# Another token order in the second half of an output projection, late mixed factors, and factor stores issued by SyncE

## The chip, the cores and the metric

The kernel runs on one core of one Trainium2 chip. Its engines are TensorE (PE, matmuls; PEld loads the stationary operand), VectorE (DVE), ScalarE (ACT), GpSimd (POOL) and SyncE (SP, which only issues transfers). Each takes its own instructions strictly in order. The metric is the device time of one execution in microseconds (us), lower is better. Three executions of the kernel before took 1875.26, 1884.01 and 1888.64 us, median 1884.01 us.

## What is computed

One layer of a hybrid encoder on 1024 tokens of width 1024, all in float32. The change touches its last third only: the output projection, the norm after it and the SwiGLU network.

```python
def reference(x, c, ...):
    ...
        merged = (jax.nn.sigmoid(ga) * (y_a @ w_branch_a[l])
                  + jax.nn.sigmoid(gb) * (y_b @ w_branch_b[l]))
        x = x + g1 * (merged @ w_out[l])

        h = rmsnorm(x, ln2_g[l]) * (1.0 + sc2) + sh2
        f = (jax.nn.silu(h @ w_ffn_gate[l]) * (h @ w_ffn_up[l])) @ w_ffn_down[l]
        x = x + g2 * f
    return x
```

The hidden width of the SwiGLU network is 2816.

## The kernel before

**Precision.** Every float32 operand of a matmul is split into a high part (a copy rounded on ACT) and a low part (source minus high part, on DVE). A product is three matmuls: high by high, high by low, low by high. `split` does this for a 128x512 weight, `split_big` for an activation factor of 128x4x512. Wherever a factor is new, PE therefore waits first for an ACT copy, then for a DVE subtraction.

**Output projection (lines 1086 to 1158).** Two passes `ch` over 512 output columns each. A pass goes over 8 token tiles `i` of 128 tokens: 24 matmuls fill one PSUM bank `e`; DVE multiplies by the gate (`tm`, line 1131) and adds the residual (`x1`, line 1138). Tiles 0 to 3 are token half 0, tiles 4 to 7 token half 1. The inputs of the projection lie in four big buffers, `mh` and `mlo` for each half. In the second pass a row of `x1` is whole, so the norm follows: ACT squares with a sum (line 1142), POOL makes the inverse root (lines 115 and 116), ACT scales into `xn` (line 1146). Two tiles later PE transposes `xn` in 8 pieces (`tail_tr`, line 1020), and `tail_ev` evicts these with scale and shift into `h2b[e][n]`, in turn on ACT (line 1030) and DVE (line 1032). Here `e` is the feature half and `n` the token half.

**Entry of the SwiGLU network.** The gate and up products run as a Strassen scheme of the Winograd kind: 7 products instead of 8 for each of the 11 pairs `j` of 128-wide weight tiles. Its seven activation factors, each split into `rh[q]` and `rl[q]`, are made of the four blocks `h2b`. Factors 0 and 1 are the raw blocks of token half 0 (buffers `bh`, `bl`, which take over big buffers of `mh` and `mlo`); 2 is the raw block of feature half 1 and token half 1; 5, 4, 6 and 3 are sums and differences. `tail_f(i)` makes the mixed blocks in place, tile by tile: part 0 has three subtractions on DVE and one ACT copy, of 128x4x128 each, part 1 two more DVE subtractions. Part 1 overwrites the raw blocks of token half 0, so factors 0 and 1 have to be split before it.

**What sets the order.** A scheduler places the instructions of each engine from the order of the code and its own estimates of time. Between `i0` (line 1113, at the last tile) and `in_order(i0)` (line 1192) each engine keeps the order in which the code was written. Buffers come in rings: 3 for `raw` weight loads, 3 for `fs`, 8 PSUM banks.

**The loop over j (lines 1255 to 1287).** `strassen(j, 0, w_g)` makes the gate and `strassen(j, 1, w_u, hidden)` the up projection. When a quadrant of their product is ready, `hidden` makes seven factors of the hidden activation, and `put_f` splits each into an `fs` buffer (ACT, then DVE) and stores it to DRAM as `d_f[q, j]`, in the order q = 0, 3, 5, 4, 6, 1, 2. ACT issues these stores, and POOL issues those of the last j (j = 10). The weights `raw` are loaded by SP.

**The down projection (from line 1289).** It walks over seven products, q = 0 first. For each (q, j) SP loads `f` from `d_f[q, j]` (`get_f`, line 1301) and PE does 12 matmuls. SP also loads the weights `wd` (line 1310).

Of the kernel before, what the change touches and what calls it, by code (L numbers as in the profile page):

```python
# [8 lines left out]
F32 = mybir.dt.float32  # L9
F32R = mybir.dt.float32r  # L10
AF = mybir.ActivationFunctionType
# [5 lines left out]
P = 128  # L17
# [11 lines left out]
def block_kernel(tc, x, x_t, cols, ada_1, ada_2, ada_row, w_q, w_kv, w_v1, w_cg, w_a, w_b, w_o, w_g, w_u, w_d, out):  # L29
# [12 lines left out]
    def big():  # L42
        return bigp.tile([P, KT, 512], F32R, tag="big", bufs=4, name=nm("big"))
# [84 lines left out]
    def tt(eng, out, a, b, op):  # L128
        eng.tensor_tensor(out=out, in0=a, in1=b, op=op)  # L129
# [346 lines left out]
    pre = {}  # L476
# [520 lines left out]
    def split(src):  # L997

        hi = wp.tile([P, 512], F32R, tag="whi", bufs=8, name=nm("whi"))
        lo = wp.tile([P, 512], F32R, tag="wlo", bufs=8, name=nm("wlo"))  # L1000
        nc.scalar.activation(hi, src, AF.Copy)
        los.append(nc.vector.tensor_tensor(out=lo, in0=src, in1=hi.bitcast(F32), op=ALU.subtract))
        return hi, lo
# [4 lines left out]
    a2 = const.tile([P, 8], F32, name="a2")  # L1008
    nc.vector.scalar_tensor_tensor(out=a2, in0=mod[:, 3, :], scalar=1.0, in1=ln2, op0=ALU.add, op1=ALU.mult)

    def split_big(dh, dl, src):
        for k in range(0, src.shape[1], 2):
            nc.scalar.activation(dh[:, k:k + 2], src[:, k:k + 2], AF.Copy)
            tt(nc.vector, dl[:, k:k + 2], src[:, k:k + 2], dh[:, k:k + 2].bitcast(F32), ALU.subtract)

    def tail_tr(xn):
        trs = [bank() for g in range(2)]
        for g in range(2):
            for j in range(4):
                nc.tensor.transpose(trs[g][:, j * P:(j + 1) * P], xn[:, (4 * g + j) * P:(4 * g + j + 1) * P], ident)  # L1020
        return trs

    def tail_ev(i, trs, acts=(0, 2)):
        n, t0 = i // 4, (i % 4) * P
        for g in range(2):
            for j in range(4):
                k = 4 * g + j
                o, s = h2b[g][n][:, j, t0:t0 + P], trs[g][:, j * P:(j + 1) * P]
                if j in acts:
                    nc.scalar.activation(o, s, AF.Identity, scale=a2[:, k:k + 1], bias=mod[:, 2, k:k + 1])  # L1030
                else:
                    nc.vector.tensor_scalar(out=o, in0=s, scalar1=a2[:, k:k + 1], scalar2=mod[:, 2, k:k + 1],
                                            op0=ALU.mult, op1=ALU.add)

    def tail_f(i, qs=(0, 1)):

        t0 = (i % 4) * P
        b = lambda e, m: h2b[e][m][:, :, t0:t0 + P]
        if 0 in qs:
            h_, l_ = (r[:, :, t0:t0 + P] for r in (rh[2], rl[2]))  # L1040
            tt(nc.vector, b(0, 1), b(0, 1), b(0, 0), ALU.subtract)
            nc.scalar.activation(h_, b(1, 1), AF.Copy)
            tt(nc.vector, l_, b(1, 1), h_.bitcast(F32), ALU.subtract)
            tt(nc.vector, b(1, 1), b(1, 1), b(0, 1), ALU.subtract)
        if 1 in qs:
            tt(nc.vector, b(0, 0), b(1, 1), b(0, 0), ALU.subtract)
            tt(nc.vector, b(1, 0), b(1, 0), b(1, 1), ALU.subtract)

    def norm2_tail(i, xn):
        tail_ev(i, tail_tr(xn))  # L1050
        if i > 3:
            tail_f(i)

    NJ = NH // 2
    pq = {}
# [4 lines left out]
    def product(w, q):  # L1060
        ps = bank()
        prod(ps, w, q)
        return ps

    def two(sa, sb):
        return product(sa, 0), product(sb, 1)
# [20 lines left out]
    for ch in range(2):  # L1087
        w = [] if ch else list(w_pre)
        for j in range(len(w) // 2, 4):
            raw = load_raw(w_o[ch, j])  # L1090
            w += [split(raw[:, c * 512:(c + 1) * 512]) for c in range(len(w) % 2, 2)]
        if ch == 0:
            ws0, ws1 = [wt(q) for q in range(4)], [wsb(q) for q in range(3)]
            for src, ws in ((w_g, ws0), (w_u, ws1 + [None])):
                w_sums(load_raw(src[0]), load_raw(src[NJ]), *ws, nc.vector)
        if ch == 1:
            swx.close()
            rqs.close()
            sr2 = ExitStack()
            r2p = sr2.enter_context(tc.tile_pool(name="phr2", bufs=1, side="right", reuse_waits="tile"))  # L1100
            rh, rl = [None] * 7, [None] * 7
            rh[2], rl[2] = (r2p.tile([P, 4, 512], F32R, name=f"r{q}2") for q in "hl")
            s5 = ExitStack()
            hp = s5.enter_context(tc.tile_pool(name="phh", bufs=1, side="right", reuse_waits="tile"))

            h2t = {q: hp.tile([P, 4, 512], F32, name=f"h2b{q}") for q in ("01", "11", "00", "10")}
            h2b = [[h2t[f"{e}{n}"] for n in range(2)] for e in range(2)]
        cs = slice(ch * 512, ch * 512 + 512)
        for i in range(8):
            n, t0 = i // 4, (i % 4) * P  # L1110
            last = (ch, i) == (1, 7)
            if last:
                i0 = len(nc.cur_bb.bb.instructions)
                s00, s00b = halves(load_raw(w_g[0]))
            xi = dp.tile([P, 512], F32, tag="xr", bufs=2, name=nm("xr"))
            nc.scalar.dma_start(xi, x[i * P:(i + 1) * P, cs])
            ps = bank()
            for k in range(KT):
                if last and k == 4:
                    trs5 = tail_tr(tails.pop(0)[1])  # L1120
                nc.tensor.matmul(ps, mh[n][:, k, t0:t0 + P], w[k][0], start=(k == 0), stop=False)
                nc.tensor.matmul(ps, mh[n][:, k, t0:t0 + P], w[k][1], start=False, stop=False)
                nc.tensor.matmul(ps, mlo[n][:, k, t0:t0 + P], w[k][0], start=False, stop=(k == KT - 1))
            if last:
                tail_ev(5, trs5)
                tail_f(5)
                pq[1] = product(s00, 0)
                trs6 = tail_tr(tails.pop(0)[1])
                pq[2] = product(s00b, 1)
            tm = dp.tile([P, 512], F32, tag="tm", bufs=1, name=nm("tm"))  # L1130
            nc.vector.tensor_tensor(out=tm, in0=ps, in1=g1b[:, cs], op=ALU.mult)
            if ch == 0:
                nc.vector.tensor_tensor(out=tm, in0=tm, in1=xi, op=ALU.add)
                nc.scalar.dma_start(d_x1[i, :, cs], tm)
                continue
            x1 = dp.tile([P, D], F32, tag="x1", bufs=2, name=nm("x1"))
            nc.scalar.dma_start(x1[:, :512], d_x1[i, :, :512])
            nc.vector.tensor_tensor(out=x1[:, cs], in0=tm, in1=xi, op=ALU.add)
            nc.scalar.dma_start(d_x1[i, :, cs], x1[:, cs])
            ss = dp.tile([P, 1], F32, tag="ss", bufs=3, name=nm("ss"))  # L1140
            xn = dp.tile([P, D], F32, tag="xn", bufs=3, name=nm("xn"))
            nc.scalar.activation(xn, x1, AF.Square, accum_out=ss)  # L1142
            r = rstd_of(ss, 1.0 / D, dp, 1)
            if last:
                s01 = halves(load_raw(w_u[0]))
            nc.scalar.activation(xn, x1, AF.Copy, scale=r[:, 0:1])
            tails.append((i, xn))
            if last:
                tail_ev(6, trs6, (0,))
                tail_f(6)  # L1150
            elif len(tails) > 2:
                norm2_tail(*tails.pop(0))
            if i == 4:
                bh, bl = big(), big()
                rh[:2], rl[:2] = (bh[:, 0:4], bh[:, 4:8]), (bl[:, 0:4], bl[:, 4:8])
            if i == 5:
                for e in range(2):
                    split_big(bh[:, 4 * e:4 * e + 4], bl[:, 4 * e:4 * e + 4], h2b[e][0])


    pre = {}
    trs7 = tail_tr(tails.pop()[1])
    s6.close()

# [4 lines left out]
    for q in (6, 3):  # L1169
        rh[q] = ep.tile([P, 4, 512], F32R, name=f"rh{q}")  # L1170
        rl[q] = ep.tile([P, 4, 512], F32R, name=f"rl{q}")
    pre[0, 1] = two(*s01)
    sp2, sp1 = split(ws0[1]), split(ws0[0])
    x1p, x11 = wt(1), wt(0)
    nc.scalar.activation(x1p, pq[1], AF.Copy)
# [6 lines left out]
    pq[6] = product(sp2, 5)  # L1182
    split_big(rh[4], rl[4], h2b[0][1])
    pq[5] = product(sp1, 4)
    tail_f(7, (1,))
    pq[3] = product(split(ws0[3]), 2)
    sp3 = split(ws0[2])
    split_big(rh[6], rl[6], h2b[0][0])
    pq[7] = product(sp3, 6)
    sp4 = split(load_raw(w_g[NJ])[:, 512:])  # L1190
    split_big(rh[3], rl[3], h2b[1][0])
    in_order(i0)
    s5.close()
# [55 lines left out]
    def put_f(q, j, src):  # L1249
        fs = cp.tile([P, 2, 512], F32R, tag="fs", bufs=3, name=nm("fs"))  # L1250
        nc.scalar.activation(fs[:, 0], src, AF.Copy)
        tt(nc.vector, fs[:, 1], src, fs[:, 0].bitcast(F32), ALU.subtract)
        (nc.gpsimd if j == NJ - 1 else nc.scalar).dma_start(d_f[q, j], fs.rearrange("p a t -> p (a t)").bitcast(F32))

    for j in range(NJ):
        gate = strassen(j, 0, w_g)
# [242 lines left out]
```

## Time and profile before

| What | us |
|---|---|
| Median of three runs (lowest, highest) | 1884.01 (1875.26, 1888.64) |
| The profiled execution, whole | 1880.62 |
| Its span, first to last instruction | 1878.8 |
| PE busy in the span | 1817.9 (97%) |
| DVE, ACT, POOL busy | 1419.7, 867.3, 371.9 |
| Mean granted TensorE clock | 0.993 |
| Second pass of the output projection | about 1176 to 1224.6 |
| Entry of the SwiGLU network | about 1224.6 to 1274.3 |
| Loop over j | to 1663.9 |
| Down projection | 1664.7 to the end |

Times in the trace count from the start of the span. A row of the timeline has the start, the duration, the engine (with a q where its queue issues a transfer), the line, the operation, the names written and read, and in brackets how long the engine had been idle and what ended that. Matmuls overlap: at the full clock one that reads 128x512 starts 0.227 us after the one before, though each is shown as 0.39 us long.

### The profile page before, as it was taken

The numbers are of one execution on the slowest core, as the hardware profiler recorded it, in microseconds if no ns is written. First come the engines' busy times: TensorE is split into PE (matmuls) and PEld (weight loads), VectorE is DVE, ScalarE is ACT, GpSimd is POOL, SyncE is SP. The second block draws the span as 40 slices with busy tenths as digits, with TensorE's granted clock in tenths as the row PEclk, the third lists the DMA queues.
The fourth block names the chain that finished last, engine by engine and source line by source line (L and its number), as shares of the span: only waits on it lengthen the run. The fifth ranks groups of instructions, "written<-read, shape, count | busy, mean of one in ns | idle before, by whom it ended". The sixth has DMA issues, their size and how long they took to land.

```text
span 1878.8 us, 24981 instructions
## 1 busy us (share of the span) xinstructions
PE 1817.9 (97%) x8813; PEld 1507.3 (80%) x8813; DVE 1419.7 (76%) x2074; ACT 867.3 (46%) x1602; POOL 371.9 (20%) x280
## 2 busy tenths in 40 slices
PE   7899999999999999999998999989999999999999
PEld 5687778888878988887886787867888888888887
DVE  6774777779865999999999544489887778744776
ACT  4442553333344777777776321564444434422321
POOL 0043327423230000000000000004544344300000
PEclk9999999999999999999999999989999999999999
DMA  9689452227748665678563536314343334379766
GB/s 389 197 311 314 172 185 79 85 74 258 268 146 261 162 193 173 172 206 269 162 176 116 203 114 218 132 66 168 146 185 141 143 134 172 135 286 351 291 227 222
DMA packets 155196, 361.62 MB, mean 192 GB/s; under 512 B 15424, under 2 KB 52544, under 8 KB 152896
## 3 DMA queue, kind: packets, MB, share of 16 engines
q1 hardware_dynamic: 80224, 237.15, 38.1%
q10 hardware_dynamic: 73840, 119.22, 17.6%
q0 software_dynamic: 1008, 3.67, 0.5%
q8 instruction: 70, 1.15, 0.2%
q14 instruction: 54, 0.44, 0.1%
HBM read 245.15 MB, written 114.82 MB: 192 GB/s over the span
## 4 chain that ended last, share of the span: by engine, by line
PE 69%; DVE 16%; DMA 6%; ACT 4%; issue 3%; POOL 1%; ACTq 0%; SPq 0%; DVEq 0%; POOLq 0%
PE e L126 6%; PE e L125 6%; PE e L124 6%; PE pj L287 5%; PE pj L124 5%; PE pj L125 5%; PE pj L126 5%; PE e L1328 4%; PE e L1327 4%; PE e L1326 4%; DVE pt L744 3%; PE pj L819 3%; PE pj L821 3%; PE pj L820 3%; PE tr L760 2%
## 5 line engine op out<-in xcount | busy, mean ns | idle before, releaser
L744 DVE TENSOR_TENSOR_SCAN pt<-pt,dm 128x128 f32<-128x128 f32 (+7 forms) x128 | 171.5, 1344 | 7.9 <-ACT pt L739 7.6
L124 PE MATMUL e<-big,whi 128*128 128x512 f32 x352 | 138.9, 395 | 2.9 <-ACT c L1227 2.0
L125 PE MATMUL e<-big,whi 128*128 128x512 f32 x352 | 138.5, 393 | 0.8 <-DVE big L129 0.8
L126 PE MATMUL e<-big,wlo 128*128 128x512 f32 x352 | 138.5, 393 | 0.0
L129 DVE TENSOR_TENSOR c<-e,c 128x512 f32<-128x512 f32 x142 | 95.4, 687 | 53.4 <-PE e L126 50.9
L115 POOL TENSOR_SCALAR rs_m<-ss 128x1 f32<-128x1 f32 x8 | 2.4, 302 | 657.9 <-ACT xn L1142 657.9
L739 ACT ACTIVATE pt<-z,rq 128x512 f32<-128x512 f32 (+1 forms) x192 | 112.5, 586 | 42.3 <-PE z L738 17.9
L124 PE MATMUL pj<-big,whi 128*128 128x512 f32 x320 | 125.1, 391 | 0.4 <-DVE c L129 0.4
L125 PE MATMUL pj<-big,whi 128*128 128x512 f32 x320 | 124.7, 390 | 0.0
L126 PE MATMUL pj<-big,wlo 128*128 128x512 f32 x320 | 124.4, 390 | 0.0
L1326 PE MATMUL e<-whi,f 128*128 128x512 f32 (+1 forms) x319 | 121.8, 382 | 0.7 <-DMA f<-d_f 0.7
L1327 PE MATMUL e<-wlo,f 128*128 128x512 f32 (+1 forms) x319 | 121.8, 382 | 0.0
L1328 PE MATMUL e<-whi,f 128*128 128x512 f32 (+1 forms) x319 | 121.7, 382 | 0.0
L287 PE MATMUL pj<-whi,big 128*128 128x512 f32 x352 | 111.9, 405 | 5.3 <-DVE vs L402 2.9
L129 DVE TENSOR_TENSOR c<-pj,c 128x512 f32<-128x512 f32 x140 | 93.3, 683 | 29.0 <-PE pj L126 28.8
L129 DVE TENSOR_TENSOR wlo<-raw,whi 128x512 fp32r<-128x512 f32 x116 | 91.5, 792 | 30.5 <-ACT whi L460 30.5
L740 ACT ACTIVATE sg<-z,rq 128x512 f32<-128x512 f32 (+1 forms) x192 | 112.5, 587 | 1.1 <-PE tr L760 1.1
L460 ACT ACTIVATE whi<-raw 128x512 fp32r<-128x512 f32 x116 | 72.8, 633 | 86.9 <-PE pj L125 38.9
L129 POOL TENSOR_TENSOR ws<-raw,raw 128x512 f32<-128x512 f32 x40 | 56.2, 1405 | 277.3 <-DMA raw<-w_cg 165.1
L764 DVE TENSOR_TENSOR atl<-tr,ath 128x512 fp32r<-128x512 f32 (+1 forms) x192 | 100.5, 543 | 6.7 <-ACT ath L763 3.7
L125 PE MATMUL e<-rl,whi 128*128 128x512 f32 x264 | 103.6, 392 | 0.4 <-DVE rl L129 0.4
L126 PE MATMUL e<-rh,wlo 128*128 128x512 f32 x264 | 103.6, 392 | 0.0
(251 smaller groups left out, 5168.5 us busy)
## 6 DMA issues: line engine op xcount, KB each, us to landing
f<-d_f SPq DMA_DIRECT2D x77, 512.0 KB, 4.3
d_f<-fs ACTq DMA_DIRECT2D x70, 512.0 KB, 3.3
raw<-w_cg SPq DMA_DIRECT2D x40, 512.0 KB, 3.8
raw<-w_g SPq DMA_DIRECT2D x25, 512.0 KB, 3.4
raw<-w_u SPq DMA_DIRECT2D x25, 512.0 KB, 3.2
ad<-ada ACTq DMA_DIRECT2D x19, 512.0 KB, 4.4
ada<-ada SPq DMA_DIRECT2D x8, 1024.0 KB, 10.1
d_t<-ts SPq DMA_DIRECT2D x16, 512.0 KB, 4.3
```

What stands on the lines that cost most here:

```text
L124: nc.tensor.matmul(ps, wh[:, k, :], fh[:, k, :], start=(k == 0), stop=False)
L125: nc.tensor.matmul(ps, wh[:, k, :], fl[:, k, :], start=False, stop=False)
L126: nc.tensor.matmul(ps, wl[:, k, :], fh[:, k, :], start=False, stop=(k == 3))
L129: eng.tensor_tensor(out=out, in0=a, in1=b, op=op)
L287: nc.tensor.matmul(ps, a, b, start=(k == 0 and q == 0), stop=(k == KT - 1 and q == 2))
L739: nc.scalar.activation(pt[:, off + s0:off + s0 + m], z[:, :m], AF.Sigmoid, scale=rq[:, 1, i, h:h + 1])
L740: nc.scalar.activation(sg[:, s0:s0 + m], z[:, :m], AF.Sigmoid, scale=rq[:, 0, i, h:h + 1])
L744: nc.vector.tensor_tensor_scan(out=pt[:, rev], data0=pt[:, rev], data1=dm[:, rev], initial=0.0, op0=ALU.mult, op1=ALU.add)
L764: nc.vector.tensor_tensor(out=tl[:, :nb, c0:c0 + P], in0=src, in1=th[:, :nb, c0:c0 + P].bitcast(F32), op=ALU.subtract)
L1326: nc.tensor.matmul(o, sh, w[0][:, c], start=(j == 0), stop=False)
L1327: nc.tensor.matmul(o, sh, w[1][:, c], start=False, stop=False)
L1328: nc.tensor.matmul(o, sl, w[0][:, c], start=False, stop=(j == NJ - 1))
```

## The change

It has four parts. (1) The second pass takes the token tiles in the order 0, 4, 1, 5, 2, 3, 6, 7. The raw factors 0 and 1, which were split whole after tile 5, are split by token tile: tiles 0 and 1 after tile 3 of the new order, tile 2 after tile 6, tile 3 inside the last tile. (2) `tail_f` keeps only its part 0 at the tiles; the two subtractions of part 1, eight of 128x4x128, are two of 128x4x512 late in the entry, one ahead of each factor made of it. (3) The two products of the first up weight, `pre[0, 1]`, stand ahead of the transposes of the last tile instead of behind them, and one weight split stands earlier. (4) All 77 stores of the factors are issued by SP.

```diff
-    def split_big(dh, dl, src):
-        for k in range(0, src.shape[1], 2):
-            nc.scalar.activation(dh[:, k:k + 2], src[:, k:k + 2], AF.Copy)
-            tt(nc.vector, dl[:, k:k + 2], src[:, k:k + 2], dh[:, k:k + 2].bitcast(F32), ALU.subtract)
+    def split_big(dh, dl, src, t=None):
+
+        if t is None:
+            cuts = [(slice(k, k + 2), slice(0, 512)) for k in (0, 2)]
+        else:
+            cuts = [(slice(0, 4), slice(t * P, t * P + P))]
+        for c in cuts:
+            nc.scalar.activation(dh[:, *c], src[:, *c], AF.Copy)
+            tt(nc.vector, dl[:, *c], src[:, *c], dh[:, *c].bitcast(F32), ALU.subtract)
...
         if i > 3:
-            tail_f(i)
+            tail_f(i, (0,))
...
-        for i in range(8):
+        for i in (0, 4, 1, 5, 2, 3, 6, 7) if ch else range(8):
...
                 if last and k == 4:
-                    trs5 = tail_tr(tails.pop(0)[1])
+                    trs3 = tail_tr(tails.pop(0)[1])
...
             if last:
-                tail_ev(5, trs5)
-                tail_f(5)
+                tail_ev(3, trs3)
+                for e in range(2):
+                    split_big(bh[:, 4 * e:4 * e + 4], bl[:, 4 * e:4 * e + 4], h2b[e][0], 3)
                 pq[1] = product(s00, 0)
                 trs6 = tail_tr(tails.pop(0)[1])
                 pq[2] = product(s00b, 1)
...
             if last:
-                tail_ev(6, trs6, (0,))
-                tail_f(6)
+                tail_ev(6, trs6)
+                tail_f(6, (0,))
             elif len(tails) > 2:
                 norm2_tail(*tails.pop(0))
-            if i == 4:
-                bh, bl = big(), big()
-                rh[:2], rl[:2] = (bh[:, 0:4], bh[:, 4:8]), (bl[:, 0:4], bl[:, 4:8])
-            if i == 5:
+            if i in (3, 6):
+                if i == 3:
+                    bh, bl = big(), big()
+                    rh[:2], rl[:2] = (bh[:, 0:4], bh[:, 4:8]), (bl[:, 0:4], bl[:, 4:8])
                 for e in range(2):
-                    split_big(bh[:, 4 * e:4 * e + 4], bl[:, 4 * e:4 * e + 4], h2b[e][0])
+                    for t in (0, 1) if i == 3 else (2,):
+                        split_big(bh[:, 4 * e:4 * e + 4], bl[:, 4 * e:4 * e + 4], h2b[e][0], t)
...
     pre = {}
+    pre[0, 1] = two(*s01)
     trs7 = tail_tr(tails.pop()[1])
...
-    pre[0, 1] = two(*s01)
...
-    tail_f(7, (1,))
-    pq[3] = product(split(ws0[3]), 2)
-    sp3 = split(ws0[2])
+    sp3, sp4 = split(ws0[3]), split(ws0[2])
+    pq[3] = product(sp3, 2)
+    tt(nc.vector, h2b[0][0], h2b[1][1], h2b[0][0], ALU.subtract)
     split_big(rh[6], rl[6], h2b[0][0])
-    pq[7] = product(sp3, 6)
+    pq[7] = product(sp4, 6)
     sp4 = split(load_raw(w_g[NJ])[:, 512:])
+    tt(nc.vector, h2b[1][0], h2b[1][0], h2b[1][1], ALU.subtract)
     split_big(rh[3], rl[3], h2b[1][0])
...
-        (nc.gpsimd if j == NJ - 1 else nc.scalar).dma_start(d_f[q, j], fs.rearrange("p a t -> p (a t)").bitcast(F32))
+        nc.sync.dma_start(d_f[q, j], fs.rearrange("p a t -> p (a t)").bitcast(F32))
```

What this does to the order of the instructions is shown at three places. The first is the queue of SP where the loop over j ends and the down projection begins. Names of the form `d_f_10` are the stores of j = 10, and `f<-d_f_0` is the load that the first matmul of the down projection needs. Before:

```order
L1310 DMA wd_15749<-w_d 128x512 x4
L1310 DMA wd_15750<-w_d 128x512 x3
L1301 DMA f_15747<-d_f_0_12242 128x1024
L1301 DMA f_15761<-d_f_1_12243 128x1024
L1301 DMA f_15764<-d_f_2_12244 128x1024
```

And now:

```order
L1318 DMA wd_15752<-w_d 128x512 x3
L1261 DMA d_f_10_12287<-fs_15665 128x1024
L1261 DMA d_f_10_12309<-fs_15693 128x1024
L1261 DMA d_f_10_12298<-fs_15697 128x1024
L1261 DMA d_f_10_12320<-fs_15702 128x1024
L1261 DMA d_f_10_12265<-fs_15725 128x1024
L1261 DMA d_f_10_12276<-fs_15730 128x1024
L1309 DMA f_15749<-d_f_0_12244 128x1024
L1309 DMA f_15763<-d_f_1_12245 128x1024
```

The six last stores of j = 10 have come from POOL's queue to SP's, and all loads of `f` stand behind them. The second place is DVE at the last token tile. Here h2b_11516 and h2b_11517 are the blocks of token half 1, h2b_11518 and h2b_11519 those of token half 0, and `tm` is what the norm of tile 7 starts from. Before:

```order
L129 TENSOR_TENSOR rl_11512<-h2b_11517,rh_11511 128x4x128
L129 TENSOR_TENSOR h2b_11518<-h2b_11517,h2b_11518 128x4x128
L129 TENSOR_TENSOR h2b_11519<-h2b_11519,h2b_11517 128x4x128
L129 TENSOR_TENSOR h2b_11517<-h2b_11517,h2b_11516 128x4x128
L129 TENSOR_TENSOR h2b_11518<-h2b_11517,h2b_11518 128x4x128
L129 TENSOR_TENSOR h2b_11519<-h2b_11519,h2b_11517 128x4x128
L1131 TENSOR_TENSOR tm_12010<-e_11925,g1b 128x512
```

And now:

```order
L129 TENSOR_TENSOR big_11847<-h2b_11518,big_11846 128x4x128
L129 TENSOR_TENSOR big_11847<-h2b_11519,big_11846 128x4x128
L1037 TENSOR_SCALAR h2b_11518<-e_11944,a_11178,mod 128x128
L1037 TENSOR_SCALAR h2b_11519<-e_11945,a_11178,mod 128x128 x2
L129 TENSOR_TENSOR big_11847<-h2b_11518,big_11846 128x4x128
L129 TENSOR_TENSOR big_11847<-h2b_11519,big_11846 128x4x128
L1137 TENSOR_TENSOR tm_12014<-e_11931,g1b 128x512
```

Mixed blocks stood ahead of `tm`; now the splits of token tiles 2 and 3 do, and the first product of the gate needs these. The third place is DVE at the end of the entry, where `rl_12065` before and `rl_12093` now belong to factor 6, `rl_12067` and `rl_12095` to factor 3. Before:

```order
L129 TENSOR_TENSOR h2b_11518<-h2b_11517,h2b_11518 128x4x128
L129 TENSOR_TENSOR h2b_11519<-h2b_11519,h2b_11517 128x4x128
L1002 TENSOR_TENSOR wlo_12191<-wt_11199,whi_12190 128x512
L1002 TENSOR_TENSOR wlo_12208<-wt_11198,whi_12207 128x512
L129 TENSOR_TENSOR rl_12065<-h2b_11518,rh_12064 128x1024 x2
L1002 TENSOR_TENSOR wlo_12231<-raw_12228,whi_12230 128x512
L1002 TENSOR_TENSOR wlo_12359<-ws_11201,whi_12358 128x512
L1002 TENSOR_TENSOR wlo_12381<-ws_11200,whi_12380 128x512
L1002 TENSOR_TENSOR wlo_12399<-ws_11202,whi_12398 128x512
L129 TENSOR_TENSOR rl_12067<-h2b_11519,rh_12066 128x1024 x2
```

And now:

```order
L1002 TENSOR_TENSOR wlo_12195<-wt_11198,whi_12194 128x512
L129 TENSOR_TENSOR h2b_11518<-h2b_11517,h2b_11518 128x2048
L129 TENSOR_TENSOR rl_12093<-h2b_11518,rh_12092 128x1024 x2
L1002 TENSOR_TENSOR wlo_12232<-raw_12229,whi_12231 128x512
L129 TENSOR_TENSOR h2b_11519<-h2b_11519,h2b_11517 128x2048
L1002 TENSOR_TENSOR wlo_12361<-ws_11201,whi_12360 128x512
L1002 TENSOR_TENSOR wlo_12383<-ws_11200,whi_12382 128x512
L1002 TENSOR_TENSOR wlo_12401<-ws_11202,whi_12400 128x512
L129 TENSOR_TENSOR rl_12095<-h2b_11519,rh_12094 128x1024 x2
```

The whole subtraction of 128x2048 now stands ahead of each of the two factors, where two of 128x4x128 stood together ahead of the first weight split.

## The prediction

> **What bounds the kernel now.** I read the busy times of the page first, then the busy time by stage, then what PE waited for, then the timeline around each wait. The first line is the page's; the others are the stages by hand: the entry up to the first split of factor 5, the rest of the entry, the end of pair j = 0, the loop, the down projection. Their columns are the stretch, its length, then busy time of PE, PEld, DVE, ACT and POOL, the granted clock, and the transfers' share and rate.
>
> ```profile
> PE 1817.9 (97%) x8813; PEld 1507.3 (80%) x8813; DVE 1419.7 (76%) x2074; ACT 867.3 (46%) x1602; POOL 371.9 (20%) x280
> ...
> 1224.56:1252.30 27.74, 21.18 (x89) 17.18 (x87) 21.66 (x40) 14.45 (x27) 0.74 (x2) 0.82 0.21 75
> 1252.30:1274.30 22.00, 19.97 (x85) 15.81 (x85) 20.95 (x28) 14.11 (x20) 2.15 (x1) 1.00 0.17 55
> 1274.30:1305.00 30.70, 28.67 (x119) 23.09 (x118) 27.97 (x36) 12.93 (x23) 19.29 (x12) 0.95 0.51 188
> 1305.00:1663.86 358.86, 358.86 (x1576) 295.57 (x1574) 281.50 (x372) 152.16 (x255) 152.15 (x105) 1.00 0.41 153
> 1663.86:1878.80 214.94, 210.45 (x958) 175.25 (x957) 127.89 (x204) 50.77 (x83) 3.20 (x6) 1.00 0.78 283
> ```
>
> PE is the bound. From 1305 to 1663.9 it has no gap at all (358.86 of 358.86), so freeing ACT there can win nothing, and only a late operand can lose. The entry is the one stage with idle PE and a lowered clock (0.82). Its waits, in total, times and longest:
>
> ```profile
> PE e L1020 <- ACT xn L1146: 6.6, 1, 6.6
> PE e L124 <- ACT c L1227: 2.0, 1, 2.0
> PE e L1326 <- DMA f<-d_f: 0.7, 1, 0.7
> ```
>
> **The change part by part: the stores on SP.** The loop ends and the down projection begins within a microsecond:
>
> ```profile
> 1663.63 0.39 PE L126 MATMUL e<-rh,wlo 128*128 128x512 f32 x1
> 1664.69 0.47 PE L1326 MATMUL e<-whi,f 128*128 128x512 f32 x1 [0.67 <-DMA f<-d_f]
> ...
> 1658.51 9.53 SPq L1301 DMA_DIRECT2D f<-d_f  x7
> ...
> 1668.00 1.29 DVE L129 TENSOR_TENSOR fs<-wt,fs 128x512 fp32r<-128x512 f32 x2
> 1669.82 0.69 DVE L129 TENSOR_TENSOR wt<-wt,c 128x512 f32<-128x512 f32 x1
> ...
> 1675.08 0.63 ACT L1251 ACTIVATE fs<-wt 128x512 fp32r<-128x512 f32 x1 [6.59 <-DMA d_f<-fs]
> ...
> d_f<-fs ACTq DMA_DIRECT2D x70, 512.0 KB, 3.3
> d_f<-fs POOLq DMA_DIRECT2D x7, 512.0 KB, 8.2
> f<-d_f SPq DMA_DIRECT2D x77, 512.0 KB, 4.3
> ```
>
> SP issued the first `f` at 1658.51, some 10 us before the stores of j = 10 were ready, so the down projection started on time while those stores were still trickling out. In the new order the load of `f` for (0, 0) stands behind the last store of j = 10 on SP, and SP can't pass a store that waits for its `fs`. So I work out when that last store can go. Stores 3 and 4 (q = 5 and 4) are ready at 1668.69 and 1669.29 as before. Store 5 takes the buffer of store 2, long free; its source is done at 1670.51, then 0.63 on ACT and 0.69 on DVE: 1671.9. Store 6 needs the buffer of store 3, which lands at 1668.75 + 3.3 = 1672.05 (the 3.3 us of ACT's 70 stores, since SP's transfers are issued like ACT's and unlike POOL's 8.2): ready at 1673.4. Store 7 needs store 4 landed (1672.65) and comes after store 6 on both engines: 1674.05. The load of `f` follows 0.4 later, at 1674.45, and takes the 4.3 us that is the median of 77: 1678.75, PE 0.15 later. Against 1664.69 that is 14.2 us of idle PE. Bounds: with the shortest landings the trace has (2.6 for a store, 3.0 for an `f`) the same sum gives 1676.75, or 12.1; with the longest store of the loop (5.3) and the 6.0 of this very load before, 1682.4, or 17.7.
>
> ```profile
> DMA to landing us min/median/max: 2.6/3.3/5.3
> ...
> DMA to landing us min/median/max: 3.0/4.3/12.1
> ...
> DMA to landing us min/median/max: 6.0/6.0/6.0
> ```
>
> A wait of that length also costs clock. After the wait of 6.6 us the pitch of matmuls was 0.427 instead of 0.227 for nine steps:
>
> ```profile
> 1237.63 1.97 PE L1020 MATMUL e<-dm,xn 128*128 128x128 f32 x8 [6.56 <-ACT xn L1146]
> 1239.25 0.78 PE L124 MATMUL e<-big,whi 128*128 128x512 f32 x1
> ...
> 1243.24 0.57 PE L124 MATMUL e<-big,whi 128*128 128x512 f32 x1
> ```
>
> From 1239.25 to 1243.24 are 3.99 us where 9 x 0.227 = 2.04 would do, a loss of 2.0 (1.6 to 2.7, counting the slow transposes or not). Together the stores cost +16.2 us, between +13.7 and +20.4. The other 70 stores cost nothing that I can find: in a round of the loop their place on SP is behind loads that were issued earlier and ahead of loads that were issued later than the store was ready:
>
> ```profile
> 1319.82 8.13 SPq L994 DMA_DIRECT2D raw<-w_g  x2
> ...
> 1321.03 0.33 ACTq L1253 DMA_DIRECT2D d_f<-fs  x1
> 1325.28 0.99 ACTq L1253 DMA_DIRECT2D d_f<-fs  x2
> ```
>
> The new queue has the load of 1319.82, these three stores, then the load of 1327.62. SP's 0.33 us an issue has room; if that cover were gone, a round could lose a wait of PE.
>
> The Trainium skill, page "DMA: Bandwidth & Descriptors", section "Issuing engines are not separate DMA queues", says that issuing from several engines only saves the sequencer's time to start a transfer. By that alone the first term would be 0 and the sum +0.3. The same page, section "Anatomy of one DMA", puts every semaphore wait on the issuing sequencer ahead of dispatch; the trace agrees with this second one, by the 2.03 us in which ACT's queue stood between two stores, below, and so I keep the first term.
>
> **The stores off ACT, end of j = 0.**
>
> ```profile
> 1297.96 2.03 ACTq L1253 DMA_DIRECT2D d_f<-fs  x2
> 1300.03 0.63 ACT L1251 ACTIVATE fs<-wt 128x512 fp32r<-128x512 f32 x1 [2.37 <-DVE fs L129]
> 1300.57 0.58 ACT L1227 ACTIVATE c<-e 128x512 f32<-128x512 f32 x1
> ...
> 1297.85 1.78 DVE L129 TENSOR_TENSOR fs<-c,fs 128x512 fp32r<-128x512 f32 x1
> ```
>
> The copy `c` for which PE waited 2.0 us stood behind a store that waited for DVE's subtraction (to 1299.63), and behind one more split. Without both it can go at 1299.65: 0.9 us saved. PE was slow after this wait too (granted clock 0.95 in that stage), a further 1.6 if the shorter wait spares it. I take -2.0, between -3.6 and 0.
>
> **The entry.** Tile 7's chain first.
>
> ```profile
> 1229.39 3.22 DVE L129 TENSOR_TENSOR h2b<-h2b,h2b 128x512 f32<-128x512 f32 x5
> 1232.53 0.68 DVE L1131 TENSOR_TENSOR tm<-e,g1b 128x512 f32<-128x512 f32 x1
> ...
> 1236.43 1.14 ACT L1146 ACTIVATE xn<-x,rs_r 128x1024 f32<-128x1024 f32 x1
> ...
> L1032 DVE TENSOR_SCALAR h2b<-e,a,mod 128x128 f32<-128x128 f32 x34 | 12.5, 407 | 8.4 <-ACT h2b L1030 8.4
> L1030 ACT ACTIVATE h2b<-e,mod,a 128x128 f32<-128x128 f32 x30 | 12.3, 450 | 6.3 <-PE e L1020 5.8 <-DVE h2b L1032 0.5
> ```
>
> The mixed subtractions leave the stretch ahead of `tm`, but the splits of tiles 2 and 3 come in, and the first gate product needs them. ACT's list there is a square with its sum (1.25), `xn` (1.14), a weight copy (0.63), six evictions (6 x 0.45) and four splits (4 x 0.63, the time of the ACT rows of L1251 above): 8.25 us from about 1220.2, so 1228.4, and DVE's last two splits end at 1228.5 and 1229.2. PE, done with the projection at 1224.56, waits until about 1228.5: a new wait of 3.9 us where there was none. `tm` moves from 1232.53 to 1229.2, and `xn` of tile 7 from 1237.57 to 1234.3, while PE now has 24 more matmuls ahead of the transposes and reaches them at about 1242: the 6.6 us wait is gone. The weights of j = 1 come next: ACT has tile 6's evictions, three copies, the table load and the Silu ahead of them, which I follow to 1243.2 and DVE's part to 1243.9, so their 24 matmuls end at 1249.0 instead of 1252.3: 3.3 us won. The slow clock after the new wait is swallowed here, PE waits for these weights anyway.
>
> ```profile
> 1252.26 3.90 ACT L1013 ACTIVATE big<-h2b 128x1024 fp32r<-128x1024 f32 x4 [1.48 <-DVE h2b L129]
> 1253.35 4.63 DVE L129 TENSOR_TENSOR big<-h2b,big 128x1024 fp32r<-128x1024 f32 x4 [1.12 <-ACT big L1013]
> 1257.89 1.29 DVE L129 TENSOR_TENSOR h2b<-h2b,h2b 128x512 f32<-128x512 f32 x2
> ...
> 1264.98 2.36 DVE L129 TENSOR_TENSOR rl<-h2b,rh 128x1024 fp32r<-128x1024 f32 x2
> ```
>
> Then DVE gives it back. A subtraction takes 0.69 us at 512 elements and 1.22 at 1024, so I estimate 2.3 at 2048. The first whole one delays factor 6: its second matmul comes at 1261.1, the product ends 2.0 us earlier than before. The second stands, with one weight split, ahead of three more weight splits and factor 3: 1262.3 + 0.6 + 2.3 + 1.9 + 1.2 = 1268.3 for its first low half, which before was there at 1266.2. PE waits some 4 us in two pieces and ends that product 1.7 us later than before, more if the clock falls. I take +2.3 for the entry, from -3.3 (the lead of 3.3 kept) to +5 (all waits followed by a slow clock). The token order itself moves no work: the same 24 matmuls a tile.
>
> The Trainium skill, "TensorE: Matmul & The Clock Gate", "Part 1: The HAM clock gate", has the clock fall after an idle window of about 3.4 us. The 2.0 us wait above was already followed by slow matmuls, so the measurement decides; by the page the two short waits of the entry would cost no clock, its term would be +1.5.
>
> **Sum.** +16.2 - 2.0 + 2.3 = +16.5 us on the profiled execution's 1880.6: 1897.1. The runs' median stands 3.4 higher, which would give 1900.5. I predict 1899.
>
> **The rivals.** (1) No hold-up: the `f` load is not late, as by the first rule of the skill above. Then -2.0 and the entry remain, and with the entry's lead kept the time is 1880.6 - 2.0 - 3.3 = 1875, not slower. For it: the page's transfers share the same 16 engines whoever issues. Against it: the order puts `f` behind the store on one queue. It decides only if the last store is ready by about 1660, 14 us before I find it. (2) The longer hold-up: the store buffers go round at 5.3 us and seven `f` loads share the rate at once, 20.4 for the first term, or the entry runs to its +5; sums of +20.7 and up, 1903 to 1909, over 1% (18.8 us). (3) Loads of `raw` caught behind waiting stores in the loop: 1 us in each of ten rounds is +10, so 1909. Against it: the rows of 1319 to 1327, where each store is ready 1.7 us or more before the next load's time. (4) The entry does what it seems to be for, at full clock: 1897.1 - 2.3 - 3.3 = 1891.5.
>
> **How the numbers follow.** My forecast has 0.50, rival 4 has 0.09, rivals 2 and 3 have 0.30 and 0.07, rival 1 has 0.04. The range takes the low ends of the first case and rival 4, and the high ends of 2 and 3: 1888 to 1909. About 1% is what a measurement of this kernel can tell from no change. The threshold of 18.8 us lies 2.3 above my sum, so slower by over 1% has 0.40 (rivals 2 and 3 and the forecast's upper edge), within 1% 0.57, faster by over 1% 0.03.
>
> **What would show it.** In the new profile PE waits 12 to 18 us for `f<-d_f` at the first matmul of the down projection, SP's first `f` load comes after the seventh store, stores land in about 3.3 us, and nine matmuls follow at the slow pitch. PE waits about 4 us ahead of the first gate product, and no longer for `xn`; it waits for factor 3's `rl`. The loop still has no gap. If PE's wait for `f` is under 5 us, the first term and the forecast are wrong; if the loop has gaps, rival 3 holds.

## The result and the profile after

The changed kernel takes 1895.34 us (median of 13 runs, 1890.15 to 1899.63); 13 runs of the kernel before now have the median 1880.39 us. The ratio is 1.0070, 95% interval 1.0059 to 1.0082: slower by 13.2 us (11.1 to 15.4). The two medians alone are 15.0 us apart; what follows goes by the ratio. The forecast was +16.5 us, and 1899 us in a range from 1888 to 1909.

The busy times of the page, after the change, are nearly those of before; PE only has a smaller share of a longer span:

```profile
PE 1821.1 (96%) x8813; PEld 1508.6 (80%) x8813; DVE 1411.0 (75%) x2070; ACT 868.0 (46%) x1608; POOL 366.8 (19%) x273
```

So no work was added; it is waiting. By stage (the stretch, its length, then busy time of PE, PEld, DVE, ACT, POOL, granted clock, share and rate of the transfers), with the entry up to the end of the products of j = 1, the rest of the entry with the end of j = 0, the loop, the down projection:

```profile
1221.01:1244.56 23.55, 20.72 (x89) 16.05 (x88) 15.92 (x30) 14.64 (x28) 0.74 (x2) 0.93 0.21 75
1244.56:1299.72 55.16, 48.91 (x203) 38.89 (x203) 49.61 (x60) 25.77 (x41) 21.19 (x12) 0.97 0.31 115
1299.72:1658.58 358.86, 358.86 (x1576) 295.49 (x1574) 279.73 (x377) 151.55 (x258) 151.64 (x105) 1.00 0.41 153
1658.58:1889.80 231.22, 212.26 (x958) 176.51 (x957) 127.53 (x203) 51.20 (x83) 0.00 (x0) 0.97 0.75 265
```

Set these beside the stretches of before. The first was 27.74 and is 4.2 shorter. The second was 22.00 + 30.70 = 52.70 and is 2.5 longer. The loop is the same to the hundredth, 358.86, without a gap. The down projection with the step into it was 214.94 and is 16.3 longer. All of the loss is in that last stage, and the list of what PE waited for names it:

```profile
PE e L1334 <- DMA f<-d_f: 15.1, 1, 15.1
...
PE e L124 <- ACT c L1235: 4.4, 2, 3.0
...
PE e L124 <- ACT big L1018: 3.5, 2, 2.4
```

The timeline of PE there, from the last matmul of the loop:

```profile
1658.34 0.39 PE L126 MATMUL e<-rh,wlo 128*128 128x512 f32 x1
...
1673.79 0.77 PE L1334 MATMUL e<-whi,f 128*128 128x512 f32 x1 [15.05 <-DMA f<-d_f]
1674.35 0.63 PE L1335 MATMUL e<-wlo,f 128*128 128x512 f32 x1
...
1677.34 0.57 PE L1336 MATMUL e<-whi,f 128*128 128x512 f32 x1
```

And SP's own row of issues in the same microseconds:

```profile
1659.00 9.52 SPq L1261 DMA_DIRECT2D d_f<-fs  x6
1668.61 21.23 SPq L1309 DMA_DIRECT2D f<-d_f  x11
```

SP stands 9.52 us over six stores that take 0.33 us each to issue. The rest is waiting for the data of each. The load that PE needs could have gone all that time (e4 below sends it 4.8 us before the last matmul of the loop); it went 0.41 us after the last store, at 1668.61, and PE started on it 5.2 us later. Behind the wait come eight matmuls at a pitch of about 0.427.

A ledger for all kernels makes such readings comparable. Each trace has the same 8813 matmuls, so I took the start of the same matmul in two traces, once in the second pass of the projection, once early in j = 0 (entry), once early in j = 1 (end of j = 0), at the last of the loop, and at the last of all. The columns give by how many us each stretch is longer than in the kernel before. The first is the drift that a trace brings along from code that no kernel here changes:

```
kernel                      drift | entry  end of j=0  loop  into and through down | sum of the four
changed                      -3.5 |  +0.4     -2.2      0.0        +16.2           |  +14.5
stores as before (e1)        -1.2 |  +2.0     -2.1      0.0         +0.5           |   +0.3
before, stores on SP (e2)    +1.4 |   0.0     -2.3      0.0        +15.8           |  +13.6
last j on POOL (e3)          +5.0 |  +2.0     -3.8      0.0         +0.4           |   -1.4
f loads on POOL (e4)         +5.1 |  +0.4     -2.4      0.0         +3.6           |   +1.6
last three on POOL (e5)      -4.4 |  +2.0     -3.8      0.0        +12.6           |  +10.8
mixed blocks early (e6)      +1.3 |  -2.3     -2.5      0.0         +0.6           |   -4.3
the same, norm late (e7)     +2.3 |  -3.6     -2.6      0.0         +0.5           |   -5.8
before, last j on POOL (e8)  +2.5 |   0.0     -2.3      0.0         +0.6           |   -1.6
```

The drift of -4.4 to +5.1 is why two profiled spans must not be subtracted here: the spans of the changed kernel and of before differ by 11.0 us, of which -3.5 belongs to nothing that was changed. The sums of the ledger, each from one trace, lie within 1.7 us of what the timed ratios give; they are taken from unrounded times.

### The profile page after: what moved, and what is told of

Its sections match the earlier page's. It is cut to its first block, busy times and chain, and to the rows that moved or that the text cites. A ratio compares the mean times of both kernels' runs of the same rounds, so it can differ in the third digit from the quotient of the medians.

```text
span 1889.8 us, 25068 instructions
## 1 busy us (share of the span) xinstructions
PE 1821.1 (96%) x8813; PEld 1508.6 (80%) x8813; DVE 1411.0 (75%) x2070; ACT 868.0 (46%) x1608; POOL 366.8 (19%) x273
## 4 chain that ended last, share of the span: by engine, by line
PE 72%; DVE 15%; DMA 5%; ACT 4%; issue 3%; POOL 0%; SPq 0%; ACTq 0%; DVEq 0%; POOLq 0%
PE e L124 6%; PE e L125 6%; PE e L126 6%; PE pj L287 5%; PE pj L124 5%; PE pj L125 5%; PE pj L126 4%; PE e L1334 4%; PE e L1335 4%; PE e L1336 4%; PE pj L819 4%; PE pj L820 4%; PE pj L821 4%; DVE pt L744 3%; PE tr L760 2%
## 5 line engine op out<-in xcount | busy, mean ns | idle before, releaser
L1334 PE MATMUL e<-whi,f 128*128 128x512 f32 (+1 forms) x319 | 122.5, 385 | 15.1 <-DMA f<-d_f 15.1
L124 PE MATMUL e<-rh,whi 128*128 128x512 f32 x264 | 103.4, 392 | 3.0 <-ACT c L1235 3.0
```

What stands on the lines that cost most here:

```text
L124: nc.tensor.matmul(ps, wh[:, k, :], fh[:, k, :], start=(k == 0), stop=False)
L1334: nc.tensor.matmul(o, sh, w[0][:, c], start=(j == 0), stop=False)
```

## The experiments

Each was timed beside the kernel before. My theory: the loss is the place of the `f` load on SP's queue, 16 us; the entry is about even; the end of j = 0 gains 2 us. The main rival: the entry costs, or SP is a bad place for stores as such.

**e1, the entry alone.** The changed kernel, with the line of the stores as before:

```diff
-        nc.sync.dma_start(d_f[q, j], ...)
+        (nc.gpsimd if j == NJ - 1 else nc.scalar).dma_start(d_f[q, j], ...)
```

> The changed kernel with the stores issued as before (ACT, and POOL for j = 10): the entry alone. Theory (the loss is the hold-up of the f load on SP, the entry is about even): +0.4 us against before, ratio 0.999 to 1.001; PE waits 0.7 us for f as before, 2 us for the copy c at the end of j = 0, about 3 us for factor 3. Rival (the entry is what costs): +5 us or more, ratio 1.003 and up.

Measured: 1880.87 us against 1881.24, ratio 0.9998 (0.9984 to 1.0011). The waits of PE in this run:

```profile
PE e L124 <- ACT c L1235: 4.4, 2, 3.0
PE e L124 <- ACT big L1018: 3.4, 2, 2.4
...
PE e L1334 <- DMA f<-d_f: 0.3, 1, 0.3
```

The waits of the entry are those of the changed kernel, the wait for `f` is gone, and so is the loss. The rival "the entry costs" falls. One detail of the theory falls too: `c` was waited for 3.0 and 1.4 us here. I had expected 2 us at the end of j = 0 with ACT issuing the stores, and the stretch gained 2.1 even so (below).

**e2, the stores alone.** The kernel before, with the opposite edit:

```diff
-        (nc.gpsimd if j == NJ - 1 else nc.scalar).dma_start(d_f[q, j], ...)
+        nc.sync.dma_start(d_f[q, j], ...)
```

> The kernel before with all 77 stores on SP, entry untouched. Theory: +16.2 for the hold-up, -2.2 at the end of j = 0, so +14 us, ratio 1.0075 (1.006 to 1.009); PE waits 14 to 16 us for the first f, and the wait for c is about 1.5 us without slow matmuls behind it. Rival (the entry is what costs): +5 us or less, ratio under 1.003.

Measured: 1897.32 us against 1881.24, ratio 1.0078 (1.0057 to 1.0099). PE's waits:

```profile
PE e L1326 <- DMA f<-d_f: 14.6, 1, 14.6
PE e L1020 <- ACT xn L1146: 6.6, 1, 6.6
PE e L124 <- ACT c L1227: 1.3, 1, 1.3
```

The old wait of 6.6 us in the entry stands, and the whole loss is there by this one line. With e1 that settles which part of the change costs.

**e3, only the last seven stores back on POOL.** The other 70 stay on SP:

```diff
-        nc.sync.dma_start(d_f[q, j], ...)
+        (nc.gpsimd if j == NJ - 1 else nc.sync).dma_start(d_f[q, j], ...)
```

> The changed kernel with only the seven stores of j = 10 back on POOL; the other 70 stay on SP. Theory: the hold-up is gone whole, the gain of 2.2 at the end of j = 0 stays: -1.8 us against before, ratio 0.999 (0.998 to 1.000); wait for f under 1.5 us, no gap in the loop. Rival (stores on SP as such cost, by its issue time or by weights that come later): +5 us or more with gaps in the loop.

Measured: 1881.80 us against 1881.24, ratio 0.9998 (0.9985 to 1.0011). The loop's stretch, and the wait for `f`, from two views:

```profile
1308.28:1667.14 358.86, 358.86 (x1576) 295.53 (x1574) 278.65 (x376) 151.50 (x258) 152.28 (x106) 1.00 0.42 155
```

```profile
PE e L1334 <- DMA f<-d_f: 0.9, 1, 0.9
```

Seven stores carried the whole loss; 70 stores on SP cost the loop nothing. The small gain that I forecast lies inside the interval and isn't shown by this run.

**e4, the stores stay, the loads move.** All 77 stores on SP, the first seven loads of `f` issued by POOL:

```diff
-        last_f[0] = nc.sync.dma_start(f..., d_f[q, j])
+        last_f[0] = (nc.gpsimd if q == 0 and j < 7 else nc.sync).dma_start(f..., d_f[q, j])
```

> The changed kernel with all 77 stores on SP, but the first seven loads of f issued by POOL, so that they stand behind no store. Theory (what holds f is its place on SP's queue): the wait falls from 15 us to under 2 us, and the time is as with the last stores on POOL, -1.8 us against before, ratio 0.998 to 1.001. Rival (f waits for the traffic of the last stores, or for buffers that come free late): PE still waits over 10 us, ratio 1.005 and up.

Measured: 1882.54 us against 1881.24, ratio 1.0006 (0.9992 to 1.0020). This is the run that tells the queue from everything else: the last stores move the same bytes through SP as in the changed kernel, and the same buffers come free. POOL's issues, and PE's matmuls that waited:

```profile
1661.86 0.76 POOL L1309 DMA_DIRECT2D f<-d_f  x1 [25.45 <-PE e L126]
1667.40 2.61 POOL L1309 DMA_DIRECT2D f<-d_f  x5 [4.78 <-PE e L126]
```

```profile
1667.55 0.47 PE L1334 MATMUL e<-whi,f 128*128 128x512 f32 x1 [0.46 <-DMA f<-d_f]
1672.59 0.77 PE L1334 MATMUL e<-whi,f 128*128 128x512 f32 x1 [2.08 <-DMA f<-d_f]
```

The first load goes early again, and the wait falls from 15.1 to 0.5. A second wait of 2.1 appears that I had not forecast. Loads 2 to 6 can only go when the loop has ended, and the second one went 0.7 us after the start of the loop's last matmul and landed 5.05 us later; in the kernel before, SP's second load went after 0.4 us and landed after 3.1. With slow matmuls behind it that is the +3.6 of the ledger. The Trainium skill, page "DMA: Bandwidth & Descriptors", section "Issuing engines are not separate DMA queues", says that starting transfers on several engines at once saves only the time on the sequencer to start them. In e4 the choice of issuer for seven loads was worth 12.6 us, because the sequencer stood in a wait; where an issuer's queue is blocked, the measurement decides against that sentence.

**e5, half of the dose.** Only the last three stores on POOL:

```diff
-        nc.sync.dma_start(d_f[q, j], ...)
+        (nc.gpsimd if j == NJ - 1 and q in (6, 1, 2) else nc.sync).dma_start(d_f[q, j], ...)
```

> The changed kernel with only the last three stores of j = 10 (q = 6, 1, 2) on POOL, the first four on SP: the first f load stands behind the fourth store. Theory (place on the queue sets the wait): in the changed kernel the fourth store went 4.8 us ahead of the seventh, so the wait for f falls from 15.1 to about 10.3 us, and the time is about +9.5 us against before, ratio 1.005 (1.0035 to 1.0065). Rival (it depends on SP carrying last stores at all, or on all of them): a wait of 15 us, or of under 2 us.

Measured: 1893.72 us against 1881.43, ratio 1.0066 (1.0053 to 1.0080), just above the range that I expected (up to 1.0065), with a wait of 12.0 us, not 10.3. SP's row and PE's:

```profile
1658.90 4.71 SPq L1261 DMA_DIRECT2D d_f<-fs  x3
1663.71 21.66 SPq L1309 DMA_DIRECT2D f<-d_f  x11
```

```profile
1657.47 0.39 PE L126 MATMUL e<-rh,wlo 128*128 128x512 f32 x1
1669.85 0.76 PE L1334 MATMUL e<-whi,f 128*128 128x512 f32 x1 [11.98 <-DMA f<-d_f]
```

The load goes 6.2 us after the last matmul of the loop instead of 10.3 (1668.61 - 1658.34), so 4.0 earlier; I had taken 4.8 from the stores alone, but the fourth store itself went 0.8 later after the end of the loop. And from issue to matmul the load needs 6.1 us instead of 5.2. The wait follows the place on the queue, neither all nor nothing. Why the store was later and the landing longer here, with three stores leaving through POOL, was not tried.

**e6, where the entry's gain went.** The entry lost its 6.6 us wait and was still even. Two new waits stand there in the changed kernel, 2.4 us before the first gate product and 3.0 before factor 3's. Here is the second on DVE and on ACT:

```profile
1257.81 2.29 DVE L129 TENSOR_TENSOR h2b<-h2b,h2b 128x2048 f32<-128x2048 f32 x1
1260.02 1.89 DVE L1002 TENSOR_TENSOR wlo<-ws,whi 128x512 fp32r<-128x512 f32 x3
1261.82 2.35 DVE L129 TENSOR_TENSOR rl<-h2b,rh 128x1024 fp32r<-128x1024 f32 x2
```

```profile
1260.13 2.00 ACT L1018 ACTIVATE rh<-h2b 128x1024 fp32r<-128x1024 f32 x2 [2.20 <-DVE h2b L129]
1262.04 0.58 ACT L1235 ACTIVATE c<-e 128x512 f32<-128x512 f32 x1
```

The whole subtraction holds up ACT's copies of factor 3, and behind these the copy `c` that frees PE's bank; PE's wait is booked on `c`, but it is the subtraction that was late. So e6 takes e3 and cuts both whole subtractions into pieces that go into gaps of DVE:

```diff
+    def part1(t0, t1):
+        b = lambda e, m: h2b[e][m][:, :, t0:t1]
+        tt(nc.vector, b(0, 0), b(1, 1), b(0, 0), ALU.subtract)
+        tt(nc.vector, b(1, 0), b(1, 0), b(1, 1), ALU.subtract)
...
             nc.vector.tensor_tensor(out=x1[:, cs], in0=tm, in1=xi, op=ALU.add)
+            if last:
+                part1(0, 256)
...
     tt(nc.vector, x11, pq[2], x1p, ALU.add)
+    part1(256, 384)
...
-    tt(nc.vector, h2b[0][0], h2b[1][1], h2b[0][0], ALU.subtract)
+    part1(384, 512)
     split_big(rh[6], rl[6], h2b[0][0])
...
-    tt(nc.vector, h2b[1][0], h2b[1][0], h2b[1][1], ALU.subtract)
     split_big(rh[3], rl[3], h2b[1][0])
```

> The changed kernel with the last seven stores on POOL, and the two late whole subtractions of the entry cut into three pieces each, put into gaps of DVE (tiles 4 and 5 behind the residual of the last tile, tile 6 behind the sum of the first gate products, tile 7 ahead of factor 6). Theory (the whole subtraction ahead of factor 3 makes PE wait there): the wait of 3.0 to 3.6 us before factor 3's product falls under 1 us, -2.5 us against the same kernel with whole subtractions, ratio to before 0.9985 (0.997 to 1.000). Rival (the early pieces only move the wait, to the first up weight or to tile 7's chain): waits there grow by 1 us or more each, ratio 1.000.

Measured: 1877.18 us against 1881.43, ratio 0.9978 (0.9966 to 0.9989). The whole interval lies below 1: it beats the kernel before and the changed one. PE's waits in its entry:

```profile
1228.39 0.49 PE L124 MATMUL e<-big,whi 128*128 128x512 f32 x1 [2.39 <-ACT big L1018]
1229.12 0.50 PE L125 MATMUL e<-big,whi 128*128 128x512 f32 x1 [0.23 <-DVE big L129]
1244.34 0.50 PE L124 MATMUL e<-big,whi 128*128 128x512 f32 x1 [0.90 <-ACT whi L1001]
1251.43 0.50 PE L124 MATMUL e<-big,whi 128*128 128x512 f32 x1 [1.07 <-ACT big L1018]
1252.69 0.50 PE L125 MATMUL e<-big,whi 128*128 128x512 f32 x1 [0.76 <-DVE big L129]
```

The wait before factor 3 is gone. The first one is that of e3; that for the weights of j = 1 fell from 1.6 to 0.9, and the pair of 1.07 and 0.76 stands where e3 had a single one of 0.5. The ledger's entry goes from +2.0 in e3 to -2.3. PE comes sooner to the end of j = 0 and waits there again, so that stretch gives 1.3 back, and the ledger's sum is 2.9 us better than in e3; 2.5 were forecast.

**e7, the other wait.** As e6, with the scaling of tile 6's norm moved behind the splits of tile 3 on ACT:

```diff
-            nc.scalar.activation(xn, x1, AF.Copy, scale=r[:, 0:1])
+            if (ch, i) == (1, 6):
+                late = (xn, x1, r)
+            else:
+                nc.scalar.activation(xn, x1, AF.Copy, scale=r[:, 0:1])
...
                     split_big(bh[:, 4 * e:4 * e + 4], bl[:, 4 * e:4 * e + 4], h2b[e][0], 3)
+                nc.scalar.activation(late[0], late[1], AF.Copy, scale=late[2][:, 0:1])
```

> As the run with the early mixed blocks, and the scaling of tile 6's norm on ACT moved behind the splits of tile 3. Theory (the first gate product waits for ACT's list): its wait of 2.4 us falls by the 1.15 us of the moved instruction to about 1.2 us; -1.2 us more, or -2.6 if the matmuls behind it stay at full clock; ratio to before 0.998 (0.9965 to 0.9995). Rival (tile 6's transposes then come late): a new wait there, no gain.

Measured: 1878.03 us against 1881.43, ratio 0.9978 (0.9966 to 0.9991), as e6. Its two waits beside those of e6:

```profile
1228.39 0.50 PE L124 MATMUL e<-big,whi 128*128 128x512 f32 x1 [1.37 <-ACT big L1018]
...
1244.35 0.50 PE L124 MATMUL e<-big,whi 128*128 128x512 f32 x1 [2.43 <-ACT whi L1001]
```

The first wait fell by 1.0 as expected; PE then ran ahead to the next one, for the weights of j = 1, which grew by 1.5. The ledger books 1.3 us for it in the entry; the timed runs show no gain over e6, so the forecast of -1.2 us more isn't shown.

**e8, the stores in the loop alone.** The kernel before, with the 70 stores on SP and the last seven on POOL:

```diff
-        (nc.gpsimd if j == NJ - 1 else nc.scalar).dma_start(d_f[q, j], ...)
+        (nc.gpsimd if j == NJ - 1 else nc.sync).dma_start(d_f[q, j], ...)
```

> The kernel before with the 70 stores of j = 0 to 9 on SP and those of j = 10 on POOL as they were. Theory (the freed copy at the end of j = 0): PE's wait there falls from 2.0 to 1.3 us and the matmuls behind it keep full clock: -2.2 us, ratio 0.9988 (0.998 to 1.0). Rival (the gain belongs to the entry's change, not to the stores): 0.

Measured: 1879.46 us against 1881.43, ratio 0.9987 (0.9978 to 0.9995), so 2.4 us faster (0.9 to 4.1). PE's wait at the end of j = 0:

```profile
PE e L124 <- ACT c L1227: 1.3, 1, 1.3
```

## Why the prediction was right, point by point

**The hold-up of `f` (forecast +14.2 and +2.0 of slow clock; measured +16.2).** Shown by e1 to e5. The working held row by row, counted from the start of the loop's last matmul (1663.63 before, 1658.34 after): by SP's single issues, store 4 was forecast at 5.7 and went at 5.05, the last at 10.4 and went at 9.9, the load at 10.8 and went at 10.3. The stores came 0.5 earlier than the sum had them, the landing took 5.2 where the sum had 4.45 with PE's start, and the two errors nearly cancel, which is luck. The bounds of 12.1 and 17.7 were set in good part by that landing, rightly: e5 shows 6.0 for the same load. (Both bounds leave out the 0.15 us for PE's start that the term itself has.)

**The other 70 stores (forecast 0; measured 0.0).** The loop is 358.86 us long in the changed kernel as in the one before. SP's rows there show it standing 5.16 us over three stores without a load of `raw` coming too late:

```profile
1317.76 0.33 SPq L994 DMA_DIRECT2D raw<-w_g  x1
1318.96 5.16 SPq L1261 DMA_DIRECT2D d_f<-fs  x3
1325.54 0.33 SPq L994 DMA_DIRECT2D raw<-w_g  x1
```

**The end of j = 0 (forecast -2.0; measured -2.2).** The size is right, the reason only in part. e8 shows the wait going from 2.0 to 1.3 by the stores alone. But e1 has the stores on ACT and gains 2.1 too: there the entry made PE 2.0 later and the copy `c` only 1.4 (it started at 1300.71, drift taken off 1302.0, against 1300.57 before), so PE waited 1.4 instead of 2.0. In each of these runs the larger piece is that no slow matmuls follow the shorter wait: before, seven of them did. The forecast had named that piece (1.6) as an if. In e3 and e5, with the stores on SP and PE 2.0 later, the wait is gone whole: -3.8.

**The entry (forecast +2.3, from -3.3 to +5; measured +0.4, and +2.0 with the same entry in e1).** The path was right, its sizes were not. The entry's term was built from the lead after the products of j = 1 (forecast 3.3, measured 4.2) and the end of factor 3's product (forecast 1.7 later than before or more; measured 0.4 later, and 1.6 in e1, where slow matmuls followed). The term that was mis-sized is the start of the second whole subtraction: the sum put it at 1262.9 (1262.3 + 0.6), and it came at 1257.81, which is 1261.3 without the drift. So factor 3 was ready 1.6 us sooner, and PE waited 3.0 us in one piece for it, not some 4 in two. That this subtraction is what it waited for, e6 shows by taking it away. The term of +1.5 without a slow clock is not worked out in the prediction; its own rows give +1.7.

A second size was wrong but is no part of the sum, because PE waits for the weights of j = 1 anyway: "a new wait of 3.9 us" before the first gate product was 2.4 in every run with the new entry but e7. I let PE wait for the last of ACT's splits of tile 3, at 1228.4, which is 1224.9 on this trace's clock, 3.5 us ahead. The trace has two splits there, and the product's first matmul, at 1223.56, went when the first was done:

```profile
1222.89 1.21 ACT L1018 ACTIVATE big<-h2b 128x512 fp32r<-128x512 f32 x2
```

The other 0.8 us is that ACT came to the end of its list, 1224.1, sooner than I had added up.

**The sum.** +16.5 was forecast, +14.5 is the ledger's sum, and +13.2 (11.1 to 15.4) what the runs show. The forecast of 1899 lies 1.9 above the sum's 1897.1, toward a median of three runs, 1884.01, that stood 3.4 above the profiled execution; 13 runs put that median at 1880.39. Rival 1 (no hold-up), rival 3 (gaps in the loop) and rival 4 (the entry's full gain) are excluded by the traces; rival 2 by the size.

## What to carry to other kernels

In these runs a transfer that waited for its data blocked everything behind it on SP's queue, even what could go at once; before moving an issue, list what stands behind it in the new queue and when its own data are ready. The price can then be added up: the time of the last wait ahead plus one landing, and here that sum came out within a microsecond, helped by two errors that cancelled. When a wait is taken away, follow PE to the next late operand: of the 6.6 us removed in the entry nothing arrived until the late subtraction was moved too, and the version with both mends, early pieces on DVE and the last seven stores on POOL (e6), is with e7 the fastest measured, 4.1 us (2.1 to 6.4) ahead of the kernel before.

## What the runs showed of the hardware that I had not expected

The slow clock behind a wait does not follow from the length of that wait. The same wait for `c` before factor 3 was 2.97 us long in the changed kernel and 2.99 in e1. Here are PE's first and last matmul of the product behind it, of the changed kernel and then of e1:

```profile
1262.67 0.50 PE L124 MATMUL e<-rh,whi 128*128 128x512 f32 x1 [2.97 <-ACT c L1235]
...
1265.53 0.39 PE L126 MATMUL e<-rh,wlo 128*128 128x512 f32 x1
```

```profile
1264.94 0.49 PE L124 MATMUL e<-rh,whi 128*128 128x512 f32 x1 [2.99 <-ACT c L1235]
...
1268.79 0.63 PE L126 MATMUL e<-rh,wlo 128*128 128x512 f32 x1
```

Eleven steps took 2.86 us in the one and 3.85 in the other, where the slow pitch set in 1.7 us after the wait had ended. The wait of 2.39 before the first gate product was followed by slow matmuls in e4 and not in e3. The Trainium skill, page "TensorE: Matmul & The Clock Gate", section "Part 1: The HAM clock gate", names an idle window of about 3.4 us before the clock falls; these waits are shorter, and the clock fell after some of them. Two waits close together (1.07 and 0.76 in the changed kernel) also had eight slow matmuls behind them. What decides between two equal waits was not tried; it makes each such wait worth up to 1.6 us more or less, which is most of the difference between the entries of +0.4 and +2.0.

Transfers issued by POOL seem to land later than those of SP: 7.6 us against 3.4 for the stores of e3, 7.0 against 3.8 for the loads of e4 (medians). But POOL's are the ones that go in the microseconds in which seven stores and seven loads crowd together. Like with like, the difference shrinks: in e4 SP's own seven last stores took 7.0, and SP's first seven loads took 5.9 in the changed kernel and 7.4 in the kernel before. So the 8.2 that the forecast put down to POOL points more to the crowd than to the issuer. In the changed kernel SP's last six stores landed after 2.6 to 3.4 us, at a time when the loads were still held. How much of the rest is POOL's own stays open.
